# Three edits in the token-mixing part of a hybrid block: diagonal scores by a constant matrix, pooling maps inside the gate's pair, half of branch B's inputs in other tiles

## The chip, the core and the metric

The kernel runs on one core of a Trainium2 chip. The core has five engines with a queue each: TensorE (PE in the profile; its weight loads are PEld), VectorE (DVE), ScalarE (ACT), GpSimd (POOL) and SyncE (SP, which issues the transfers). Each works through its own instructions in their order and waits for the others by semaphores. The metric is device time in microseconds (us) of one execution, lower is better. Before, three timed executions took 2380.71, 2383.26 and 2383.93 us.

## The reference, cut to what matters

One layer over 1024 tokens of width 1024: a half-step FFN, a token-mixing part, a second half-step FFN and a gated embedding. The change lies in the mixing part.

```python
h = _rmsnorm(x, mix_norm[i])
proj = h @ w_in[i]
q_r, f_r, i_r, og_r, pool_r, ga_r, gb_r = jnp.split(proj, split_points, axis=-1)
f = lb + (1.0 - lb) * jax.nn.sigmoid(f_r)
k = 1.0 - f
q = jax.nn.silu(q_r)                      # 8 heads of 128
# branch A, per head:  S_t = diag(f_t) S_{t-1} + k_t outer v_t,   o_t = S_t^T q_t
o = _hgrn2_chunked(q, k, v, log_f)
o = _rmsnorm(o, hgrn_onorm[i]) * jax.nn.silu(og_r)
y_a = o @ w_branch_a[i]
# branch B: trailing means over 2/4/8/16 tokens minus the token, then a map per group of 128 channels
pooled = _causal_multiscale_pool(u)       # u: pool_r in 4 groups
mixed = jnp.einsum('bsgc,gcd->bsgd', pooled, pool_w[i]) * pool_scale[i]
y_b = mixed @ w_branch_b[i]
x = x + (jax.nn.sigmoid(ga_r) * y_a + jax.nn.sigmoid(gb_r) * y_b) @ w_out[i]
```

Within a chunk, token t's own contribution to o_t is (q_t . k_t) v_t. This number, the score of a token with itself, stands on the diagonal of the score matrix.

## The kernel before

**Arithmetic.** Every f32 operand of a large product is split into a rounded part and a remainder (`split`, line 117: a cast on ACT, line 118, and a subtraction on DVE, line 119). A product is three matmuls of 128x512 (`mm3`, lines 157 to 159: high by high, high by low, low by high). Names that end in h and l are the two parts.

**Pairs.** Two weight blocks that meet the same activations are multiplied together by a seven-product scheme (`pair`). Its weight parts are `wa` (from tile `ra`, loaded), `ws` (sums `s` made on POOL, lines 90 and 93), `wd` and `wt` (from `rb`, loaded and then overwritten by POOL). The order on PE is: products 1 and 2 (24 matmuls, into banks pA and pC, with `wa`), the two products that the pair before left over (`flushed`), then 6, 5 and 7 into pA, pB and pA. Behind product 7, ACT copies pA (line 386) and DVE adds pB (line 81). A pair takes 84 matmuls.

**Pools.** SBUF tiles come from pools: `a` (28 tiles 128x1024, activation parts), `w` (12 tiles, weights and their parts, means and pooling parts), `q`, `u` and `h` (smaller). PSUM has three banks pA, one pB, one pC and three `aux`. A tile that is asked for waits until the one whose place it takes has been read for the last time.

**Heads.** For each of 8 heads, `hgrn(h, half)` (line 916) works on two halves of 512 tokens, in 12 groups of small PE work (scores of a token with itself at line 930; scores of blocks of 1, 2, 4 ... 64 tokens at line 946, with q and k multiplied by running products of f on DVE between them; transposes of v and k at 977 and 986; the state at 994; the output at 1015 and 1017). Then the head's output is normed: squares on ACT (1020), `rstd` (a sum on DVE, a power on POOL, lines 168 and 169), a multiplication on DVE (1022). The groups of a head are interleaved with the pairs that run beside it (`among`): each head has two or three pairs beside it, and these define how many matmuls lie between two groups. `head(h)` takes the first step of `hgrn` only when head h begins.

**What is ordered by whom.** PE's order is the order of the program (`manual_schedule`). The queues of the other engines are ordered by the tile scheduler when the kernel is built.

**Pooling.** Beside heads 0 and 2, `pool_pair` makes two groups' inputs, `beside_means` makes the trailing means on DVE beside the next pair, and `pool_maps` (line 875) multiplies each of four blocks with its 128x128 map (`pb` by `pwhl`, three matmuls each, into `aux`), scales it on ACT and stores it to `m_dram`. After that comes the gate's pair `gate_pair`.

**Branch B.** `act_b` (line 1089) loads the four mixed groups back into tiles `m` and splits them into eight `a` tiles; `branch_b` multiplies them during the end of head 7 and after it; and `load_act` loads the heads' outputs and makes the activation parts (x0, x3, xT1, xT3) for branch A's pairs, also in `a` tiles.

Of the kernel before, what the change touches and what calls it, by code (L numbers as in the profile page):

```python
# [9 lines left out]
F32R = mybir.dt.float32r  # L10
# [4 lines left out]
ALU = mybir.AluOpType  # L15

P = 128
# [6 lines left out]
HEADS = 8  # L24
# [13 lines left out]
def hybrid_block(ctx: ExitStack, tc: tile.TileContext, a: dict, out: bass.AP):  # L38
# [16 lines left out]
    nc = tc.nc  # L55
# [11 lines left out]
    def t_(tag, s, dt=F32):  # L67
        n, bufs = ROOM[tag]
        return sb.tile([P, n], dt, tag=tag, name=name(s), bufs=bufs)

    def bank(tag, s=None):
        return psum.tile([P, HALF], F32, tag=tag, name=name(s or tag), bufs=BANKS[tag])
# [13 lines left out]
    def mul(o, x, y):  # L86
        nc.vector.tensor_tensor(o, x, y, ALU.mult)
# [10 lines left out]
    mhalf = small("mhalf", [P, NT])  # L98
    nc.vector.memset(mhalf, -0.5)
    masks = {}  # L100
    for h in LEVELS[:5]:

        n = 64 // h
        m = small(f"mask{h}", [P, n], BF16)
# [16 lines left out]
    def hilo(src, tag, s):  # L121

        n = src.shape[1]
        hi, lo = t_(tag, s + "h", F32R)[:, :n], t_(tag, s + "l", F32R)[:, :n]
        split(src, hi, lo)
        return hi, lo

    def hilo_half(src, tag, s):

        t = t_(tag, s, F32R)  # L130
        n = src.shape[1]
        hi, lo = t[:, :n], t[:, HALF : HALF + n]
        split(src, hi, lo)
        return hi, lo

    def halves(hl, m=HALF):

        n = hl[1].shape[1] // m
        return [(hl[0][:, c], hl[1][:, c]) for c in (slice(i * m, (i + 1) * m) for i in range(n))]
# [12 lines left out]
    def store(dst, src):  # L152
        latest[0] = nc.sync.dma_start(out=dst, in_=src).ins

    def mm3(ps, ah, al, bh, bl, first, last):
        kw = {"skip_group_check": True}
        nc.tensor.matmul(ps, ah, bh, start=first, stop=False, **kw)  # L157
        nc.tensor.matmul(ps, ah, bl, start=False, stop=False, **kw)  # L158
        nc.tensor.matmul(ps, al, bh, start=False, stop=last, **kw)  # L159

    def chunks(t, n=4):
        return [t[:, c * P : (c + 1) * P] for c in range(n)]
# [239 lines left out]
    def steps(it, n=9):  # L402
        for end in it:
            n -= end
            if not n:
                return
# [234 lines left out]
    def two_halves(s, n):  # L641
# [3 lines left out]
    ga_dram, gb_dram, yb_dram, y_dram = (  # L645
        two_halves(s, KC) for s in ("ga_dram", "gb_dram", "yb_dram", "y_dram")
    )
    m_dram = two_halves("m_dram", NG)
# [9 lines left out]
    ps = bank("pA")  # L658
# [28 lines left out]
    parts, gp = [], []  # L687
# [65 lines left out]
    pscale = load(small("pscale", [P, NG]), a["pool_scale"])  # L753
# [4 lines left out]
    Q, F, V, OG, PU, GA, GB = 0, 8, 16, 24, 32, 36, 44  # L758
    heads = {}

    def qf_pair(h):
        qk, f = [t_("q", "qk") for _ in range(2)], [t_("u", "f") for _ in range(2)]
        heads[h] = qk, f

        made = set()

        def k_(half):
            if half in made:
                nc.scalar.activation(qk[half][:, R], f[half], AF.Copy, scale=-1.0, bias=1.0)
            made.add(half)  # L770

        def q_(half):
            def go(q):
                k = qk[half][:, R]
                nc.scalar.activation(k, q, AF.Sigmoid)
                mul(q, q, k)
                k_(half)
            return go

        def f_(half):  # L780
            def go(src):
# [55 lines left out]
    def beside_means(it):  # L837

        for part in it:
            yield part  # L840
            while means and next(means[0], 0) == 0:
                means.pop(0)
        while means:
            for _ in means.pop(0):
                pass
# [29 lines left out]
    def pool_maps():  # L875

        r = t_("h", "pwr")
        load(r.rearrange("p (g d) -> p g d", g=NG), a["pool_w"].rearrange("g c d -> c g d"))
        wh, wl = hilo_half(r, "w", "pwhl")
        todo = [(g, half, u[half]) for g, u in pooled for half in range(2)]  # L880
        pooled.clear()
        parts = [hilo_half(u, "w", "pb") for _, _, u in todo[:3]]
        for _ in range(5):
            yield False
        for i, (g, half, u) in enumerate(todo):
            gc = slice(g * P, (g + 1) * P)
            if i + 3 < len(todo):
                parts.append(hilo_half(todo[i + 3][2], "w", "pb"))
            ps = bank("aux")
            mm3(ps, wh[:, gc], wl[:, gc], *parts.pop(0), True, True)  # L890
            nc.scalar.mul(u, ps, pscale[:, g : g + 1])
            store(m_dram[g][half], u)
            yield False

    def pool_pair(g):
        got = {}

        def done(i, half, t, src):
            if src is not t:
                nc.scalar.copy(t, src)  # L900
            got[i, half] = t
            for k in range(2):
                if (k, 0) in got and (k, 1) in got:
                    means.append(pool_means(g + k, [got.pop((k, 0)), got.pop((k, 1))]))

        yield from out_pair(w_in[PU + g], w_in[PU + g + 1], act, done)
# [9 lines left out]
    def hgrn(h, half):  # L916
# [5 lines left out]
        qk, f = heads[h][0][half], heads[h][1][half]  # L922
        q, k = qk[:, L], qk[:, R]
        qc, kc = chunks(q), chunks(k)
        sc = scores[half]
        yield

        ps = bank("aux")
        for p_, k_, q_ in zip(chunks(ps), kc, qc):
            nc.tensor.matmul(p_, k_, q_, start=True, stop=True)  # L930
        mul(q, q, f)
        nc.vector.copy_predicated(
            sc, ident.bitcast(U32).unsqueeze(1).to_broadcast([P, 4, P]),
            ps.rearrange("p (c t) -> p c t", c=4),
        )

        tots = {1: f}
        tot = t_("h", "tot")
        for hh in LEVELS:
            yield  # L940
            n = 64 // hh
            ps = bank("aux").rearrange("p (c x) -> p c x", c=4)
            m = 64 if hh == 64 else P
# [6 lines left out]
            by = view(tots[hh], 0, [[1, 2], [2, na], [0, hh]])  # L950
# [24 lines left out]
        ps = bank("aux")  # L975
# [8 lines left out]
        ps = bank("aux")  # L984
# [52 lines left out]
    GROUPS = 12  # L1037
    turns = []

    def head(h):  # L1040

        two = [hgrn(h, half) for half in range(2)]
        for it in two:
            next(it)
        for i in range(GROUPS):
            for it in two:
                next(it, None)
            if i in (1, 2) and turns:
                turns.pop(0)()
            yield  # L1050

    def among(its, groups, n):

        parts = (p for it in its for p in it if not p)
        done = 0
        for i, _ in enumerate(groups, 1):
            while done * GROUPS < i * n:
                next(parts, None)
                done += 1
        for k, _ in enumerate(parts):  # L1060
            if k in (1, 4) and turns:
                turns.pop(0)()
# [3 lines left out]
    def around(first, acts, *its):  # L1066
        yield first
        next(acts)
        for it in its[:-1]:
# [2 lines left out]
        yield its[-1]  # L1072

    more = {
        0: lambda: (pool_pair(0), beside_means(qf_pair(1)), pool_maps(),
                    gate_pair(GB, 0, gb_dram)),
        2: lambda: (pool_pair(2), beside_means(qf_pair(3)), pool_maps(),
                    gate_pair(GB, 2, gb_dram)),
        4: lambda: (qf_pair(5), gate_pair(GB, 4, gb_dram), gate_pair(GB, 6, gb_dram)),
        6: lambda: (qf_pair(7), gate_pair(GA, 0, ga_dram), gate_pair(GA, 2, ga_dram)),  # L1080
        7: lambda: around(gate_pair(GA, 4, ga_dram), act_b(), gate_pair(GA, 6, ga_dram), flushed(),
# [1 line left out]
    }  # L1083
    for it in (v_pair(0), qf_pair(0), og_pair(0)):
        steps(it)

    m_parts = []

    def act_b():
        behind[0] = latest[0]  # L1090
        for g in range(NG):
            m = t_("q", "m")
            for half, c in enumerate((L, R)):
                load(m[:, c], m_dram[g][half])
            m_parts.append(halves(hilo(m, "a", "m")))
        m_last, behind[0] = latest[0], None
        yield True
        behind[0] = m_last
        yield True

# [13 lines left out]
    with tc.manual_schedule(engines={nc.tensor.engine}):  # L1114
        for h in range(HEADS):
            its = more[h]() if h in more else (v_pair(h + 1), qf_pair(h + 1), og_pair(h + 1))
            among(its, head(h), (66 if h == 7 else 3 * PAIR + 9 * (h in (0, 2))))
        while turns:
            turns.pop(0)()
    behind[0] = og_last[0]  # L1120
# [275 lines left out]
```

## Time and profile before

| | |
|---|---|
| time, median of three | 2383.26 us (2380.71 to 2383.93) |
| the profiled execution's own time | 2379.58 us |
| its span | 2377.9 us |
| PE busy | 97% of the span |
| DVE, ACT, POOL busy | 61%, 41%, 19% |
| mean granted TensorE clock | 0.993 |
| diagonal scores (line 930), PE records | 128, 15.6 us busy |

A row of a timeline reads: start in us from the span's start, duration in us, engine, line, operation, out<-in, shapes, how many instructions the row holds, and in brackets how long the engine had been idle before it and what ended that. A matmul's duration is modelled and overlaps the next one's, so the pace is read from the starts. A row of a group of instructions ends with busy us and mean ns, then the idle time before them with its releasers. A row of the windows reads: from:to, length, busy us (count), granted clock, share of the DMA engines, GB/s.

### The profile page before, as it was taken

To read this page: it belongs to the slowest core of one execution; us is meant where nothing else is said; L and a number is where in the kernel's file an instruction comes from. 1 tells how busy PE (TensorE), PEld (TensorE's weight loads), DVE (VectorE), ACT (ScalarE), POOL (GpSimd) and SP (SyncE) were. 2 spreads that over 40 slices of the span, in tenths; PEclk is the share of its full clock that TensorE was granted. 3 is DMA by queue.
4 is the path that set the end of the run, shared out by engine and by line. 5 is a ranking of instruction groups with operands and counts; after the bars stand their busy time and mean duration, and the time that the engine had idled before them with its cause. 6 is when DMAs were issued, how large, how long until landed. Compare 5 with 4: busy or idle time off the path is not lost.

```text
span 2377.9 us, 29405 instructions
## 1 busy us (share of the span) xinstructions
PE 2311.8 (97%) x11058; PEld 1915.3 (81%) x11058; DVE 1457.7 (61%) x2037; ACT 980.3 (41%) x1528; POOL 442.8 (19%) x397
## 2 busy tenths in 40 slices
PE   8999999999999999999999998999999999999997
PEld 6778887888877888788888887877787888888886
DVE  6555555467656766676557567677454544568568
ACT  7344333333554333333433343346333333334656
POOL 1333222200012132122222202102223222000000
PEclk9999999999999999999999999999999999999999
DMA  4345444493431232232232366761343523754334
GB/s 183 133 139 174 152 167 140 139 347 108 138 122 58 77 106 72 80 98 84 80 99 76 98 229 230 259 229 45 109 148 124 182 93 107 263 212 131 102 97 151
DMA packets 133759, 331.75 MB, mean 140 GB/s; under 512 B 15216, under 2 KB 16240, under 8 KB 133616
## 3 DMA queue, kind: packets, MB, share of 16 engines
q1 hardware_dynamic: 133616, 329.87, 40.6%
q8 instruction: 87, 1.43, 0.3%
q14 instruction: 56, 0.46, 0.1%
HBM read 228.62 MB, written 101.19 MB: 139 GB/s over the span
## 4 chain that ended last, share of the span: by engine, by line
PE 71%; DVE 10%; DMA 7%; ACT 4%; issue 4%; POOL 4%; SPq 1%; POOLq 0%; DVEq 0%; ACTq 0%
PE pA L157 11%; PE pA L159 11%; PE pA L158 11%; PE pB L157 5%; PE pB L158 5%; PE pB L159 5%; PE aux L946 4%; PE pC L159 3%; PE pC L157 3%; PE pC L158 3%; PE aux L158 2%; PE aux L159 2%; PE aux L157 2%; DMA rb<-in_ffn_w_dram 2%; POOL s L90 1%
## 5 line engine op out<-in xcount | busy, mean ns | idle before, releaser
L90 POOL TENSOR_TENSOR s<-rb 128x512 f32<-128x512 f32 x74 | 99.5, 1344 | 836.5 <-DMA rb<-in_ffn_w_dram 352.4
L119 DVE TENSOR_TENSOR wtl<-rb,wth 128x1024 fp32r<-128x1024 f32 x74 | 90.7, 1225 | 169.3 <-ACT wth L118 169.3
L118 ACT CAST wsh<-s 128x1024 fp32r<-128x1024 f32 x74 | 77.9, 1053 | 233.9 <-POOL s L93 192.4
L119 DVE TENSOR_TENSOR wsl<-s,wsh 128x1024 fp32r<-128x1024 f32 x74 | 90.9, 1229 | 122.4 <-ACT wsh L118 122.4
L93 POOL TENSOR_TENSOR rb<-ra,s 128x512 f32<-128x512 f32 x74 | 96.4, 1303 | 341.9 <-DVE wd L119 328.6
L118 ACT CAST wth<-rb 128x1024 fp32r<-128x1024 f32 x74 | 77.7, 1050 | 194.5 <-POOL rb L93 191.1
L119 DVE TENSOR_TENSOR wal<-ra,wah 128x1024 fp32r<-128x1024 f32 x74 | 91.5, 1238 | 94.9 <-PE pC L158 50.8
L118 ACT CAST gh<-gr 128x1024 fp32r<-128x1024 f32 x84 | 81.8, 981 | 144.0 <-PE aux L158 86.3
L119 DVE TENSOR_TENSOR gl<-gr,gh 128x1024 fp32r<-128x1024 f32 x84 | 94.9, 1133 | 71.7 <-ACT gh L118 69.5
L118 ACT CAST wah<-ra 128x1024 fp32r<-128x1024 f32 x74 | 77.7, 1051 | 127.7 <-DMA ra<-in_ffn_w_dram 96.7
L157 PE MATMUL pA<-xT3h,wth 128*128 128x512 f32 x296 | 117.7, 398 | 10.6 <-ACT g L383 8.0
L157 PE MATMUL pA<-xT1h,wsh 128*128 128x512 f32 x280 | 112.0, 400 | 9.4 <-ACT xT1h L118 7.4
L157 PE MATMUL pB<-xT1h,wsh 128*128 128x512 f32 x296 | 118.2, 399 | 2.8 <-DVE o L81 1.1
L157 PE MATMUL pA<-x0h,wah 128*128 128x512 f32 x296 | 118.1, 399 | 0.8 <-ACT x0h L118 0.8
L158 PE MATMUL pA<-x0l,wah 128*128 128x512 f32 x296 | 115.7, 391 | 2.0 <-DVE x0l L119 2.0
L157 PE MATMUL pB<-x,wth 128*128 128x512 f32 x296 | 117.2, 396 | 0.0
L159 PE MATMUL pA<-xT3h,wtl 128*128 128x512 f32 x296 | 116.0, 392 | 0.5 <-DVE wtl L119 0.5
L158 PE MATMUL pB<-xT1l,wsh 128*128 128x512 f32 x296 | 116.1, 392 | 0.3 <-DVE xT1l L119 0.3
L159 PE MATMUL pB<-xT1h,wsl 128*128 128x512 f32 x296 | 116.2, 393 | 0.0
L158 PE MATMUL pA<-xT3l,wth 128*128 128x512 f32 x296 | 116.1, 392 | 0.0
L159 PE MATMUL pA<-x0h,wal 128*128 128x512 f32 x296 | 115.6, 391 | 0.0
L159 PE MATMUL pC<-x0h,wal 128*128 128x512 f32 x296 | 115.4, 390 | 0.0
(342 smaller groups left out, 6538.9 us busy)
## 6 DMA issues: line engine op xcount, KB each, us to landing
ra<-in_ffn_w_dram SPq DMA_DIRECT2D x47, 512.0 KB, 3.7
rb<-in_ffn_w_dram SPq DMA_DIRECT2D x44, 512.0 KB, 3.7
gsS<-gs SPq DMA_DIRECT2D x88, 256.0 KB, 2.2
rB<-in_ffn_w_dram SPq DMA_DIRECT2D x40, 512.0 KB, 6.8
gr<-gsS SPq DMA_DIRECT2D x40, 512.0 KB, 3.4
gsA<-g SPq DMA_DIRECT2D x66, 256.0 KB, 2.0
gr<-gsA SPq DMA_DIRECT2D x30, 512.0 KB, 5.8
ra<-in_w_in_dram SPq DMA_DIRECT2D x27, 512.0 KB, 3.7
```

What stands on the lines that cost most here:

```text
L90: nc.gpsimd.tensor_tensor(o, x, y, ALU.add)
L93: nc.gpsimd.tensor_tensor(o, x, y, ALU.subtract)
L118: nc.scalar.copy(hi, src)
L119: nc.vector.tensor_tensor(lo, src, hi.bitcast(F32), ALU.subtract)
L157: nc.tensor.matmul(ps, ah, bh, start=first, stop=False, **kw)
L158: nc.tensor.matmul(ps, ah, bl, start=False, stop=False, **kw)
L159: nc.tensor.matmul(ps, al, bh, start=False, stop=last, **kw)
L946: nc.tensor.matmul(ps[:m, c, :64], kc[c][:, :m], right, start=True, stop=True)
```

## The change

It has three parts.

1. **Diagonal scores.** Before, four 128x128 products k^T q in f32 per half gave all pairs of tokens, of which the diagonal was taken. Now DVE multiplies −2 q by k element by element (`tot`), splits that, and two 128x512 matmuls with a 128x128 matrix of −0.5 (one column of `mhalf`, broadcast) sum it over the 128 channels, so that every row holds the diagonal. This step and the first multiplication of q by f now stand in `hgrn`'s first step, and `begin_head` takes this step for head h+1 in the last group of head h (for head 0 ahead of all heads).
2. **Pooling maps.** All four blocks are split at once, and the maps are now multiplied inside the gate's pair, behind its first 24 matmuls (`maps_beside`). Scaled blocks go to tiles `mo` of the `w` pool.
3. **Branch B's inputs.** Two of the four groups are split into `w` tiles in place of `a` tiles.

```diff
@@ pool_maps
-        wh, wl = hilo_half(r, "w", "pwhl")
         todo = [(g, half, u[half]) for g, u in pooled for half in range(2)]
         pooled.clear()
-        parts = [hilo_half(u, "w", "pb") for _, _, u in todo[:3]]
-        for _ in range(5):
-            yield False
-        for i, (g, half, u) in enumerate(todo):
-            gc = slice(g * P, (g + 1) * P)
-            if i + 3 < len(todo):
-                parts.append(hilo_half(todo[i + 3][2], "w", "pb"))
-            ps = bank("aux")
-            mm3(ps, wh[:, gc], wl[:, gc], *parts.pop(0), True, True)
-            nc.scalar.mul(u, ps, pscale[:, g : g + 1])
-            store(m_dram[g][half], u)
+        parts = [hilo_half(u, "w", "pb") for _, _, u in todo]
+        wh, wl = hilo_half(r, "w", "pwhl")
+        ms = [m for _ in range(2) for m in halves((t_("w", "mo"),) * 2)]
+        yield
+        for (g, half, _), hl in zip(todo, parts):
+            gc = slice(g * P, (g + 1) * P)
+            ps = bank("aux")
+            mm3(ps, wh[:, gc], wl[:, gc], *hl, True, True)
+            m = ms.pop(0)[0]
+            nc.scalar.mul(m, ps, pscale[:, g : g + 1])
+            store(m_dram[g][half], m)
             yield False
+    def maps_beside(it):
+        maps = pool_maps()
+        next(maps)
+        done = 0
+        for part in it:
+            yield part
+            done += not part
+            if part and done == 8:
+                yield from maps
@@ hgrn
+        tot = t_("h", "tot")
+        nc.vector.scalar_tensor_tensor(tot, q, -2.0, k, ALU.mult, ALU.mult)
+        hi, lo = hilo_half(tot, "w", "qkk")
+        mul(q, q, f)
         yield
         ps = bank("aux")
-        for p_, k_, q_ in zip(chunks(ps), kc, qc):
-            nc.tensor.matmul(p_, k_, q_, start=True, stop=True)
-        mul(q, q, f)
+        by = mhalf[:, :1].bitcast(F32R).to_broadcast([P, P])
+        kw = {"skip_group_check": True}
+        nc.tensor.matmul(ps, by, hi, start=True, stop=False, **kw)
+        nc.tensor.matmul(ps, by, lo, start=False, stop=True, **kw)
@@ head
+    begun_heads = {}
+
+    def begin_head(h):
+        begun_heads[h] = [hgrn(h, half) for half in range(2)]
+        for it in begun_heads[h]:
+            next(it)
+
     def head(h):
-        two = [hgrn(h, half) for half in range(2)]
-        for it in two:
-            next(it)
+        two = begun_heads.pop(h)
         for i in range(GROUPS):
...
+            if i == GROUPS - 1 and h + 1 < HEADS:
+                begin_head(h + 1)
             yield
@@ more
-        0: lambda: (pool_pair(0), beside_means(qf_pair(1)), pool_maps(),
-                    gate_pair(GB, 0, gb_dram)),
+        0: lambda: (pool_pair(0), beside_means(qf_pair(1)),
+                    maps_beside(gate_pair(GB, 0, gb_dram))),
@@ act_b
             for half, c in enumerate((L, R)):
                 load(m[:, c], m_dram[g][half])
-            m_parts.append(halves(hilo(m, "a", "m")))
+            ms.append(m)
         m_last, behind[0] = latest[0], None
+        m_parts.extend(halves(hilo(m, "a", "m")) for m in ms[:2])
         yield True
+        m_parts.extend(halves(hilo(m, "w", "m")) for m in ms[2:])
```

Head 2's line changes as head 0's does, and the count of parts beside heads 0 and 2 goes from 3 x 28 + 9 to 3 x 28 + 4. Line numbers behind the edits move by up to 14: 946 becomes 960, 986 becomes 1000, 994 becomes 1008, 1020 becomes 1034, 1022 becomes 1036, and 932 becomes 947.

The edits change the queues of the other engines too. Three places follow; a row is line, operation, out<-in, shape.

DVE's queue at the start of head 0, before: `wal` belongs to the first pair beside head 0 (`wal_6032`), `o_5495` is the output of the pair ahead of it, `qk` and `f` are the two halves' q, k and f.

```order
L119 TENSOR_TENSOR wal_6032<-ra_6029,wah_6031 128x1024
L783 TENSOR_SCALAR f_5492<-f_5492,lb_126,lb 128x512
L87 TENSOR_TENSOR qk_5490<-qk_5490 128x512
L783 TENSOR_SCALAR f_5491<-f_5491,lb_126,lb 128x512
L119 TENSOR_TENSOR wsl_6041<-s_1189_6037,wsh_6040 128x1024
L119 TENSOR_TENSOR wd_6044<-rb_6035,wd_6044 128x512
L119 TENSOR_TENSOR wtl_6050<-rb_6035,wth_6049 128x1024
L81 TENSOR_TENSOR o_5495<-o_5495,pB_5963 128x512
L87 TENSOR_TENSOR qk_5489<-qk_5489,f_5491 128x512
L932 COPY_PREDICATED score_5481<-ident,aux_6009 128x512
```

The same place now:

```order
L81 TENSOR_TENSOR o_5495<-o_5495,pB_5963 128x512
L938 SCALAR_TENSOR_TENSOR tot_6007<-qk_5489 128x512
L938 SCALAR_TENSOR_TENSOR tot_6013<-qk_5490 128x512
L87 TENSOR_TENSOR o_5495<-o_5495,sg_6003 128x512
L119 TENSOR_TENSOR qkk_6009<-tot_6007,qkk_6009 128x512
L87 TENSOR_TENSOR qk_5489<-qk_5489,f_5491 128x512
L119 TENSOR_TENSOR qkk_6015<-tot_6013,qkk_6015 128x512
L87 TENSOR_TENSOR qk_5490<-qk_5490,f_5492 128x512
L947 COPY_PREDICATED score_5481<-ident,aux_6021 128x512
L947 COPY_PREDICATED score_5482<-ident,aux_6025 128x512
L87 TENSOR_TENSOR tot_6007<-f_5491 128x256
L119 TENSOR_TENSOR wal_6036<-ra_6033,wah_6035 128x1024
```

The products `tot` and their remainders stand behind the sum of `o`, and `wal` of the first pair has moved from ahead of all these to behind the two masked copies of the diagonal.

ACT's queue around the maps of head 2, before: `pb` and `pwhl` are the parts of the means and of the map, `wah`, `wsh` and `wd` belong to the gate's pair, L978 and L987 are the copies of v and k after their transposes, L891 scales a map.

```order
L118 CAST pb_7738<-o_7298 128x512
L118 CAST pb_7741<-o_7299 128x512
L891 ACTIVATE o_7301<-aux_7744,pscale 128x512
L118 CAST wah_7786<-ra_7784 128x1024
L978 COPY v_7466<-aux_7750 128x512
L978 COPY v_7476<-aux_7756 128x512
L891 ACTIVATE o_7300<-aux_7762,pscale 128x512
L891 ACTIVATE o_7298<-aux_7768,pscale 128x512
L891 ACTIVATE o_7299<-aux_7774,pscale 128x512
L118 CAST wsh_7795<-s_1445_7792 128x1024
L118 CAST wd_7799<-rb_7790 128x512
L987 COPY qk_6893<-aux_7828 128x512
```

The same place now (L992, L1001 and L890 are those copies and the scaling):

```order
L118 CAST pwhl_7755<-pwr_7741 128x512
L118 CAST wah_7766<-ra_7764 128x1024
L992 COPY v_7474<-aux_7802 128x512
L992 COPY v_7484<-aux_7808 128x512
L365 COPY o_7760<-pC_7789 128x512
L118 CAST wsh_7775<-s_1449_7772 128x1024
L830 ACTIVATE o_7760<-o_7760 128x512
L118 CAST wd_7779<-rb_7770 128x512
L1001 COPY qk_6903<-aux_7842 128x512
L1001 COPY qk_6904<-aux_7850 128x384
L118 CAST wth_7784<-rb_7770 128x1024
L890 ACTIVATE mo_7758<-aux_7830,pscale 128x512
```

Before, the maps were scaled ahead of `wsh`; now `wsh`, `wd`, the copies of k and `wth` stand ahead of the first scaling.

DVE's queue at the same place, before, where L868 makes the last of the means:

```order
L868 SCALAR_TENSOR_TENSOR o_7299<-pw_7711,o_7299 128x512
L119 TENSOR_TENSOR pwhl_7729<-pwr_7727,pwhl_7729 128x512
L119 TENSOR_TENSOR pb_7732<-o_7301,pb_7732 128x512
L119 TENSOR_TENSOR pb_7735<-o_7300,pb_7735 128x512
L119 TENSOR_TENSOR pb_7738<-o_7298,pb_7738 128x512
L119 TENSOR_TENSOR pb_7741<-o_7299,pb_7741 128x512
L119 TENSOR_TENSOR wal_7787<-ra_7784,wah_7786 128x1024
```

The same place now, with the remainder of the map behind those of the means:

```order
L868 SCALAR_TENSOR_TENSOR o_7313<-pw_7725,o_7313 128x512
L119 TENSOR_TENSOR pb_7743<-o_7315,pb_7743 128x512
L119 TENSOR_TENSOR pb_7746<-o_7314,pb_7746 128x512
L119 TENSOR_TENSOR pb_7749<-o_7312,pb_7749 128x512
L119 TENSOR_TENSOR pb_7752<-o_7313,pb_7752 128x512
L119 TENSOR_TENSOR pwhl_7755<-pwr_7741,pwhl_7755 128x512
L119 TENSOR_TENSOR wal_7767<-ra_7764,wah_7766 128x1024
```

`wal` of the gate's pair follows them as it did before; what moved is PE's first use of it, from behind the maps to ahead of them.

More of the change, by code (lines that the diff above doesn't have):

```diff
@@ L937, in hgrn @@
         tots = {1: f}
-        tot = t_("h", "tot")
         for hh in LEVELS:
@@ L1074, in hybrid_block @@
     more = {
-        0: lambda: (pool_pair(0), beside_means(qf_pair(1)), pool_maps(),
-                    gate_pair(GB, 0, gb_dram)),
-        2: lambda: (pool_pair(2), beside_means(qf_pair(3)), pool_maps(),
-                    gate_pair(GB, 2, gb_dram)),
+        0: lambda: (pool_pair(0), beside_means(qf_pair(1)),
+                    maps_beside(gate_pair(GB, 0, gb_dram))),
+        2: lambda: (pool_pair(2), beside_means(qf_pair(3)),
+                    maps_beside(gate_pair(GB, 2, gb_dram))),
         4: lambda: (qf_pair(5), gate_pair(GB, 4, gb_dram), gate_pair(GB, 6, gb_dram)),
@@ L1085, in hybrid_block @@
         steps(it)
+    begin_head(0)
     m_parts = []
@@ L1090, in act_b @@
         behind[0] = latest[0]
+        ms = []
         for g in range(NG):
@@ L1116, in hybrid_block @@
             its = more[h]() if h in more else (v_pair(h + 1), qf_pair(h + 1), og_pair(h + 1))
-            among(its, head(h), (66 if h == 7 else 3 * PAIR + 9 * (h in (0, 2))))
+            among(its, head(h), (66 if h == 7 else 3 * PAIR + 4 * (h in (0, 2))))
         while turns:
```

## Prediction

> **What bounds the kernel now.** I read the page's span and busy shares first.
>
> ```profile
> span 2377.9 us, 29405 instructions
> PE 2311.8 (97%) x11058; PEld 1915.3 (81%) x11058; DVE 1457.7 (61%) x2037; ACT 980.3 (41%) x1528; POOL 442.8 (19%) x397
> ```
>
> PE is busy in all but 66 us of the span. A matmul removed is therefore time won, and a wait of PE that an edit adds is time lost in full, unless it was waiting there already. So after the count of matmuls the question is which of PE's operands come late in the new order. Next I read PE's timeline at the start of head 0.
>
> ```profile
> 775.11 0.39 PE L159 MATMUL pA<-xT3h,wtl 128*128 128x512 f32 x1
> 775.34 1.95 PE L930 MATMUL aux<-qk 128*128 128x128 f32 x16
> 777.04 0.48 PE L157 MATMUL pA<-x0h,wah 128*128 128x512 f32 x1
> 777.35 0.40 PE L158 MATMUL pA<-x0l,wah 128*128 128x512 f32 x1
> 777.58 0.39 PE L159 MATMUL pA<-x0h,wal 128*128 128x512 f32 x1
> ```
>
> A 128x512 matmul follows the one before after 0.23 us. The 16 records of L930 hold PE for 1.70 us, and the matmul behind them takes 0.08 more than that pace.
>
> **Edit 1, the diagonal scores.** Out go 1.78 us in each of 8 heads; in come four matmuls of 0.227 us, so 0.91: **−7.0**. Weights that are one column read 128 times stand in no row of before. From below, they can't beat the pace, for which each product still streams 512 columns. From above, if they ran like L930 (1.70 us for 1024 columns), a head's 2048 columns would take 3.4 us, 20 us more over all heads. I take the pace, for the nearest rows in type and width have it, and keep the 20 as the far end.
>
> The price stands in the queues. The four matmuls need the new product `tot`, its cast (ACT) and its remainder (DVE), and each engine works through its queue in order. Head 0 first, with the rows of ACT and DVE there, and the group of `wal`:
>
> ```profile
> 777.59 0.58 ACT L386 COPY o<-pA 128x512 f32<-128x512 f32 x1
> ...
> 778.86 0.68 DVE L81 TENSOR_TENSOR o<-o,pB 128x512 f32<-128x512 f32 x1
> 779.46 0.69 DVE L87 TENSOR_TENSOR qk<-qk,f 128x512 f32<-128x512 f32 x1
> 780.06 0.75 DVE L932 COPY_PREDICATED score<-ident,aux 128x512 f32<-128x512 uint32 x1
> ```
>
> ```profile
> L119 DVE TENSOR_TENSOR wal<-ra,wah 128x1024 fp32r<-128x1024 f32 x74 | 91.5, 1238 | 94.9 <-PE pC L158 50.8 <-ACT wah L118 30.3 <-issue 8.4
> ```
>
> In the new order DVE's sum of `o` with pB stands ahead of both products `tot`. That sum waits for ACT's copy of pA, and the copy for PE's matmul at 775.11, the one directly ahead of the diagonal. So PE has to stop. The matmul is done at 775.5, the copy at 776.2; then the sum and seven more DVE operations of 512 at 0.60 each (the step from 778.86 to 779.46) reach 781.0, two masked copies, which now stand ahead of `wal` and wait for the diagonal itself, some 782.3, a first total 782.6, and `wal` with its 1.24 us 783.9. PE needs `wal` for the third matmul behind the diagonal, at 775.34 + 0.91 + 0.45 = 776.7. **+7.2** in head 0, in pieces of about 2.9, 2 and 2.3 us: before the diagonal, between its matmuls, and before `wal`. In before `wal` lay ahead of all this, and nothing waited.
>
> At the other seven starts `wal` of the head's first pair has moved behind both norms of the head before:
>
> ```profile
> 855.00 0.17 DVE L168 TENSOR_SCALAR rso<-rso 128x4 f32<-128x4 f32 x1
> ...
> 856.30 0.69 DVE L1022 TENSOR_TENSOR qk<-aux,rso 128x512 f32<-128x512 f32 x1 [1.02 <-POOL rso L169]
> ...
> 857.48 1.95 PE L930 MATMUL aux<-qk 128*128 128x128 f32 x16
> ...
> 931.11 0.17 DVE L168 TENSOR_SCALAR rso<-rso 128x4 f32<-128x4 f32 x1 [3.17 <-ACT qk L1020]
> ...
> 936.33 1.95 PE L930 MATMUL aux<-qk 128*128 128x128 f32 x16
> ...
> 1021.85 0.16 DVE L168 TENSOR_SCALAR rso<-rso 128x4 f32<-128x4 f32 x1
> ...
> 1024.98 1.95 PE L930 MATMUL aux<-qk 128*128 128x128 f32 x16
> ```
>
> Behind the first `rso` now stand POOL's power (1.3 us from `rso` to norm), the norm, a remainder (0.6 each), a total (0.4), the second power and norm (1.3 and 0.6), five small totals (0.6 in all) and `wal` (1.2): 6.6 us. PE wants `wal` 1.36 us after the diagonal begins. In head 2 that is 5.22 + 1.36 = 6.6 us after `rso`: 0.2 us of waiting at most, and DVE's idle 3.17 us ahead of `rso` take up the new operations that stand before it; heads 4 to 7 begin alike. In head 1 there are only 2.48 + 1.36 = 3.8 us. The queue ahead of its `rso` loses `wsl` and `wal` and gains five operations of 0.6, and I let `rso` come 0.3 earlier: +2.5. Head 3 has 3.13 + 1.36, so +1.7. With 0.2 for the other five, **+5.2** (from 0 to 12).
>
> **Edit 2, the pooling maps.**
>
> ```profile
> 992.59 0.62 ACT L118 CAST pb<-o 128x512 fp32r<-128x512 f32 x1 [0.48 <-DVE o L868]
> 993.07 2.49 DVE L119 TENSOR_TENSOR pb<-o,pb 128x512 fp32r<-128x512 f32 x4
> 993.81 0.80 PE L158 MATMUL aux<-pb,pwhl 128*128 128x512 f32 x1 [3.86 <-DVE pb L119]
> ...
> 995.71 1.03 ACT L118 CAST wah<-ra 128x1024 fp32r<-128x1024 f32 x1
> ```
>
> ```profile
> 985.00:993.00 8.00, 4.87 (x31) 1.00 0.36 116
> 993.00:1000.00 7.00, 6.19 (x19) 0.52 0.46 152
> ```
>
> ```profile
> 827.44 0.39 PE L157 MATMUL aux<-pb,pwhl 128*128 128x512 f32 x1
> ```
>
> (In the windows the second number is PE's busy time, the one behind the count its granted clock.) PE's wait of 3.86 us in head 2 goes, and the clock of 0.52 behind it, at which 6.19 us were spent on matmuls that need half: **−3.9 and −3.0**. But the gate's own matmuls now stand where the first map stood, and their `wah` and `wal` stand in ACT's and DVE's queues behind the casts and remainders of the means. In head 2 the last mean ends at 992.6. ACT then casts pb, pwhl and `wah` (to 994.7); DVE makes the five remainders at 0.60 and `wal` (to 996.7). PE's third matmul wants `wal` at 989.9: **+6.85**, first 5.3 and then 1.5. In head 0 the means are early, but `wah` waits behind the copy of `f`, whose product has just ended at 827.4: 0.6 + 1.05 + 1.24 us, less 0.45 for two matmuls that need `wah` alone: **+2.55**.
>
> Then the maps. Between them stand the transposes of k, and the copies that free their banks stand in ACT's queue behind `wsh`, a gate value and `wd` of the gate's pair:
>
> ```profile
> 999.87 1.28 POOL L90 TENSOR_TENSOR s<-rb 128x512 f32<-128x512 f32 x1 [37.91 <-DMA rb<-in_w_in_dram]
> ...
> 1002.55 1.05 ACT L118 CAST wsh<-s 128x1024 fp32r<-128x1024 f32 x1 [1.56 <-POOL s L93]
> ```
>
> Tile `s` takes the place that `wah` gives back, so POOL can begin only when the gate's first 24 matmuls end. From there `wsh` comes after 2.7 us (999.87 to 1002.55), the first copy after 2.0 more, and takes 0.5: 5.2. PE has 1.6 us of work by then (two maps, four transposes): a wait of 3.6. The second copy adds 0.6. The fourth map's bank waits for the first scaled map, which stands behind `wth` on ACT, which waits for POOL's last sum, and that for `wd`: 1.5. Together 5.7 in each of two heads: **+11.4** (from 0 to 14). The 24 matmuls ahead are no cover, since the chain begins with their end.
>
> **Edit 3, branch B's inputs.**
>
> ```profile
> 1456.53 0.50 PE L157 MATMUL pA<-x0h,wah 128*128 128x512 f32 x1 [0.81 <-ACT x0h L118]
> ...
> 1458.59 0.50 PE L158 MATMUL pA<-x0l,wah 128*128 128x512 f32 x1 [1.55 <-DVE x0l L119]
> ...
> 1463.58 0.50 PE L157 MATMUL pA<-xT3h,wsh 128*128 128x512 f32 x1 [1.71 <-DVE o L81]
> ...
> 1469.11 0.50 PE L158 MATMUL pA<-xT3l,wsh 128*128 128x512 f32 x1 [1.70 <-DVE xT3l L119]
> ```
>
> ```profile
> 1440.48 0.45 SPq L149 DMA_DIRECT2D rb<-in_w_branch_a_dram  x1
> ```
>
> These 5.8 us and 0.3 for xT1l between them end when four `a` tiles are free. In their place `rb` stands behind one more store in SP's queue, some 1.4 us later; `wsh`, `wd` and `wth` move with it, and the copy of pC stands behind `wth` on ACT, so that the sum which frees pA ends at about 1460.6, where PE is at 1458.5: +2.1. Left is **−4.0** (from −1.5 to −6).
>
> **The clock.** Before has another drop, in this place:
>
> ```profile
> 747.20 0.79 PE L157 MATMUL pA<-xT1h,wsh 128*128 128x512 f32 x1 [2.46 <-ACT xT1h L118]
> ```
>
> ```profile
> 747.00:751.00 4.00, 3.80 (x10) 0.57 0.38 100
> ```
>
> A wait of 2.46 us was enough for about 4 us at 0.57, which costs some 1.5 us. Head 0's start, head 2's gate and both rows of maps wait as long in the new order: **+6** for the four (from 0 to 12, with a second stretch behind each). The Trainium skill, "TensorE: Matmul & The Clock Gate", section "HAM oscillation", asks for "no PE-idle gaps >~3.4µs". This trace has a drop after 2.46, so here the measurement decides; by the rule the term would be about 3.
>
> **Sum**, on the profiled 2379.58: −7.0 −4.0 −3.9 −3.0 +7.2 +5.2 +6.85 +2.55 +11.4 +6.0 = +21.3, so 2400.9. That execution lies 3.7 below the median of the three timed ones; I add 1.5 for this: **2402.4**.
>
> **Rivals.** (1) The new work is ready before PE: then the savings alone are left, −17.9, about 2364. For it speaks DVE's 61% busy; against it, that in head 0 the chain hangs on PE's own last matmul. It decides if `wal` ends before 776.7 there and before 989.9 in head 2. Chance 0.14. (2) The maps find their banks: if `s` needn't wait for `wah`, 11.4 goes and half the clock's term with it: 2388. 0.11. (3) Only the longest wait drops the clock, as the 3.86 did, so head 2's gate would and the others wouldn't, save for parts of the maps: term 3, 2399. 0.09. (4) The broadcast weights run like L930: 2422. 0.04. The forecast has 0.62.
>
> **Numbers.** A measurement can tell about 0.2%, 4.8 us. Faster by more: 0.14, from (1). Within: 0.07, from (2), whose 2388 lies at the edge. Slower: 0.79. The range goes from 2378, which leaves out (1) alone, up to 2417, where clock and starts reach for their upper ends.
>
> **What would show it.** Right: PE idle for some 3 and 2 us at head 0's first L945 and L946; 5 us before the gate's first matmul in head 2, released by `wah`; waits before the transposes (L1000) and the last map; none over a microsecond for x0 and xT3 at the end of the mix. Wrong: L945 and the maps without waits, or L945 above 0.25 us apiece.

## The result, and the profile after

| | before | after |
|---|---|---|
| time, median of four | 2382.77 us (2380.71 to 2383.93) | 2441.42 us (2438.61 to 2443.18) |
| ratio | | 1.0249, 95% interval 1.0235 to 1.0262 |
| span of the profiled execution | 2377.9 us | 2441.5 us |
| mean granted TensorE clock | 0.993 | 0.981 |

The change made the kernel 58.7 us slower. The direction was forecast, the size was not: +19, and at most +34, had been expected. The page of the changed kernel begins like this (busy us, share of the span, instructions):

```profile
span 2441.5 us, 29225 instructions
PE 2331.4 (95%) x10962; PEld 1921.5 (79%) x10962; DVE 1490.5 (61%) x2069; ACT 986.3 (40%) x1544; POOL 443.0 (18%) x397
```

PE has 96 instructions fewer in the records and is busy for 20 us longer, and the span has grown by 64. So PE waits more, and it runs part of the time at a lower clock. The timeline of head 0's start, which answers to the first rows of the prediction:

```profile
776.94 0.51 PE L945 MATMUL aux<-qkk,mhalf 128*128 128x512 f32 x1 [2.65 <-ACT qkk L118]
778.09 0.49 PE L946 MATMUL aux<-qkk,mhalf 128*128 128x512 f32 x1 [0.65 <-DVE qkk L119]
...
779.29 0.79 PE L946 MATMUL aux<-qkk,mhalf 128*128 128x512 f32 x1 [0.47 <-DVE qkk L119]
...
782.58 0.80 PE L159 MATMUL pA<-x0h,wal 128*128 128x512 f32 x1 [1.64 <-DVE wal L119]
```

These are the three pieces that were foreseen: a wait before the diagonal, waits between its matmuls, one for `wal`; 5.4 us in all. The start of head 4 was to cost 0.2 us. The timeline of all engines there:

```profile
1141.93 1.29 POOL L90 TENSOR_TENSOR s<-rb 128x512 f32<-128x512 f32 x1
1141.99 0.69 DVE L1036 TENSOR_TENSOR qk<-aux,rso 128x512 f32<-128x512 f32 x1 [0.90 <-POOL rso L169]
...
1142.60 3.44 DVE L87 TENSOR_TENSOR tot<-tot 128x64 f32<-128x64 f32 x4
1142.93 0.40 PE L945 MATMUL aux<-qkk,mhalf 128*128 128x512 f32 x1
...
1143.30 1.29 POOL L93 TENSOR_TENSOR s<-s,ra 128x512 f32<-128x512 f32 x1
...
1144.55 1.26 POOL L93 TENSOR_TENSOR rb<-ra,rb 128x512 f32<-128x512 f32 x1
1146.07 0.16 DVE L87 TENSOR_TENSOR lbr<-tot 128x4 f32<-128x4 f32 x1
1146.15 1.23 DVE L119 TENSOR_TENSOR wal<-ra,wah 128x1024 fp32r<-128x1024 f32 x1
...
1147.43 0.50 PE L159 MATMUL pA<-x0h,wal 128*128 128x512 f32 x1 [2.95 <-DVE wal L119]
```

Four small totals of f, of 64, 32, 16 and 8 elements, take 3.44 us, and they take them while POOL makes its three sums. Behind them stands `wal`, and PE waits 2.95 us for it. The waits for `wal` at the starts of heads 1 to 7 are 2.51, 2.95, 3.49, 2.95, 3.45, 2.95 and 3.33 us, 21.6 together. The granted clock there, by windows of 3.4 us (from:to, length, then busy us of PE, weight loads, DVE, ACT and POOL, granted clock, DMA share, GB/s):

```profile
1141.10:1144.50 3.40, 3.39 (x15) 2.44 (x13) 2.47 (x3) 0.59 (x1) 3.32 (x3) 1.00 0.00 0
1144.50:1147.90 3.40, 0.47 (x2) 0.43 (x3) 3.30 (x6) 0.00 (x0) 1.31 (x2) 1.00 0.00 0
1147.90:1151.30 3.40, 3.40 (x10) 2.62 (x9) 3.11 (x5) 2.09 (x3) 0.00 (x0) 0.50 0.14 52
1151.30:1154.70 3.40, 3.40 (x19) 2.87 (x18) 0.75 (x2) 1.05 (x1) 1.29 (x1) 1.00 0.07 25
```

A window in which PE idles for 2.93 us is followed by one at half clock. PE's timeline there shows the pace:

```profile
1148.94 0.63 PE L157 MATMUL pA<-x0h,wah 128*128 128x512 f32 x1
1149.37 0.63 PE L158 MATMUL pA<-x0l,wah 128*128 128x512 f32 x1
```

Matmuls start 0.43 us apart in place of 0.23, so about half of such a window is lost, some 1.6 us. In the mixing part the clock is at a half for 20 such windows, against 3 before. Last, the gate of head 2, its maps, and the end of the mix, from PE's timeline:

```profile
1017.97 0.80 PE L157 MATMUL pA<-x0h,wah 128*128 128x512 f32 x1 [5.36 <-ACT wah L118]
...
1033.63 0.55 PE L1000 MATMUL aux<-ident,qk 128*128 128x128 f32 x3 [3.34 <-ACT qk L1001]
1034.74 0.50 PE L157 MATMUL aux<-pb,pwhl 128*128 128x512 f32 x1 [0.57 <-ACT qk L1001]
...
1037.05 0.80 PE L157 MATMUL aux<-pb,pwhl 128*128 128x512 f32 x1 [1.06 <-ACT mo L890]
...
1522.74 0.50 PE L157 MATMUL pA<-xT3h,wsh 128*128 128x512 f32 x1 [4.51 <-DVE o L81]
```

The gate's 5.4 us and the maps' 3.3, 0.6 and 1.1 are near what was forecast (5.3; 3.6, 0.6 and 1.5). The wait of 4.5 us for `o`, where branch A begins, was to be 2.1.

### The profile page after: what moved, and what is told of

The parts are those of the page before. It is cut to its first block, busy times and chain, and to the rows that moved or that the text cites. A ratio compares the mean times of both kernels' runs of the same rounds, so it can differ in the third digit from the quotient of the medians.

```text
span 2441.5 us, 29225 instructions
## 1 busy us (share of the span) xinstructions
PE 2331.4 (95%) x10962; PEld 1921.5 (79%) x10962; DVE 1490.5 (61%) x2069; ACT 986.3 (40%) x1544; POOL 443.0 (18%) x397
## 4 chain that ended last, share of the span: by engine, by line
PE 68%; DVE 11%; DMA 8%; ACT 4%; issue 4%; POOL 4%; SPq 1%; POOLq 0%; DVEq 0%; ACTq 0%
PE pA L157 11%; PE pA L159 11%; PE pA L158 10%; PE pB L157 5%; PE pB L158 5%; PE pB L159 5%; PE aux L960 4%; PE pC L159 3%; PE pC L157 3%; PE pC L158 3%; DMA rb<-in_ffn_w_dram 2%; PE aux L157 2%; PE aux L159 2%; PE aux L158 2%; POOL s L90 1%
## 5 line engine op out<-in xcount | busy, mean ns | idle before, releaser
L159 PE MATMUL pA<-x0h,wal 128*128 128x512 f32 x296 | 121.1, 409 | 24.6 <-DVE wal L119 24.6
L157 PE MATMUL pC<-x0h,wah 128*128 128x512 f32 x296 | 119.1, 402 | 0.0
L158 PE MATMUL pC<-x0l,wah 128*128 128x512 f32 x296 | 118.5, 400 | 0.0
L157 PE MATMUL pA<-xT3h,wd 128*128 128x512 f32 x280 | 113.1, 404 | 3.6 <-ACT c L386 2.6
```

## Experiments

Each was timed against the kernel before on the same chip, whose own median lay between 2378 and 2381 us there. Ratios are to that kernel, with their 95% intervals.

### The three edits, one at a time

`e1_diag_alone` is the kernel before with the first edit and nothing else:

```diff
+        nc.vector.scalar_tensor_tensor(tot, q, -2.0, k, ALU.mult, ALU.mult)
+        hi, lo = hilo_half(tot, "w", "qkk")
+        mul(q, q, f)
...
+            if i == GROUPS - 1 and h + 1 < HEADS:
+                begin_head(h + 1)
```

> The kernel before with the diagonal scores of the change alone (edit 1). Theory A (from the profile of the changed kernel: 5.4 us of waits at the start of head 0, 21.6 us for wal at the other seven starts, and about ten stretches of 3.4 us at half clock, less 7 us of matmuls): 2410 to 2425 us, with wal waited for 2.5 to 3.5 us in each of seven heads. Rival B (the waits at the starts of heads 1 to 7 come from the maps and branch B's tiles, which share the pool w with the parts of the product; alone, the edit costs what the forecast said, about +5): 2383 to 2393 us.

`e2_maps_alone` has the second edit only:

```diff
-        0: lambda: (pool_pair(0), beside_means(qf_pair(1)), pool_maps(),
-                    gate_pair(GB, 0, gb_dram)),
+        0: lambda: (pool_pair(0), beside_means(qf_pair(1)),
+                    maps_beside(gate_pair(GB, 0, gb_dram))),
```

> The kernel before with the maps inside the gate's pair alone (edit 2). Theory A (waits of 9.7 us at the rows of maps, 8.3 us at the gates' starts, less 3.9, and eight stretches of 3.4 us at half clock in place of two): about 2402 to 2412 us. Rival B (the gates' and maps' operands come late only because edit 1 holds DVE and ACT there): 2375 to 2388 us.

`e3_branch_b_alone` has the third:

```diff
+        m_parts.extend(halves(hilo(m, "a", "m")) for m in ms[:2])
         yield True
+        m_parts.extend(halves(hilo(m, "w", "m")) for m in ms[2:])
```

> The kernel before with half of branch B's inputs in w tiles alone (edit 3). Theory A (the splits of the heads' outputs, which now find their tiles early, stand ahead of the gb multiplications on DVE, so that yb's banks and rb come later; 4.5 us of waiting before the first pair of branch A and one stretch at half clock; the saving is eaten up): 2381 to 2388 us. The forecast's step (rb 1.4 us later): 2379 us, four less than before.

| edit | time, median | ratio | forecast for it (with its share of the clock) |
|---|---|---|---|
| 1, diagonal | 2418.12 us | 1.0160 (1.0142 to 1.0178) | +6.9 us |
| 2, maps | 2398.67 us | 1.0078 (1.0059 to 1.0097) | +18.4 us |
| 3, branch B | 2378.45 us | 0.9997 (0.9988 to 1.0006) | −4.0 us |

Before had 2378.97 us on this chip, so the edits give +39.2, +19.7 and −0.5, which add up to 58.3 of the 58.7 of the whole. The times in the expectations go by the 2383 us of before on the first chip; as differences to before, all three runs lie where Theory A had them (+27 to +42, +19 to +29, and −2 to +5). Edit 2's time came out as forecast, its terms less so (below). The loss that was not forecast is in edit 1, some 32 us, with the waits for `wal` at the seven starts also when it is alone (2.94 to 3.46 us). It needs neither the maps nor the other tiles.

### What makes `wal` late at heads 1 to 7

`e4_totals_behind` leaves the changed kernel as it is, but queues the totals behind the masked copy on DVE. This sets an order and adds no wait:

```diff
-        nc.vector.copy_predicated(
+        cp = nc.vector.copy_predicated(
...
-            mul(tots[2 * hh], pv[:, :, 0], pv[:, :, 1])
+            with tc.issue_after(cp.ins):
+                mul(tots[2 * hh], pv[:, :, 0], pv[:, :, 1])
```

> The changed kernel, with the totals of f queued on DVE behind the masked copies of the diagonal, so that they are no longer ahead of wal. Theory A (each small total on DVE waits for one of POOL's three sums, so that four totals take 3.4 us in place of 0.9, and this is nearly all of the 2.95 to 3.5 us that PE waits for wal): wal is waited for under 1.2 us at heads 1 to 7, and the time falls by 15 to 33 us, to 2408 to 2426 us. Rival B (wal is late by the two powers and norms ahead of it and by its own cast, whatever the totals do): the waits stay within 0.8 us of 3, and the time within 8 us of 2441.

Measured: 2406.93 us, ratio 1.0112 (1.0097 to 1.0128), against the changed kernel's 1.0249, a difference of 33 us and the far end of what Theory A expected (15 to 33). The start of head 4 in this run:

```profile
1127.98 1.70 DVE L119 TENSOR_TENSOR wal<-ra,wah 128x1024 fp32r<-128x1024 f32 x1
...
1128.67 2.16 POOL L93 TENSOR_TENSOR s<-s,ra 128x512 f32<-128x512 f32 x1
...
1130.18 0.39 PE L159 MATMUL pA<-x0h,wal 128*128 128x512 f32 x1
```

PE no longer waits for `wal` at the start of any of heads 1 to 7, and no window at half clock is left there. `wal` (1.70 us against 1.23) and POOL's second sum (2.16 against 1.29) still lengthen each other, but there is time for it.

This run takes the totals away from `wal` as well as from POOL's sums. `e5_sums_behind_wal` holds the other side fixed: DVE's queue is that of the changed kernel, instruction by instruction, and POOL's sums come later.

```diff
+            if fresh:
+                fresh.clear()
+                lo = w["A11"][1].bitcast(F32)
+                held = nc.gpsimd.tensor_tensor(dummy, lo[:, :1], lo[:, :1], ALU.add).ins
+                with tc.issue_after(held):
+                    pool_add(s[:, L], rb[:, L], rb[:, R])
...
                 begin_head(h + 1)
+                fresh.append(True)
```

> The changed kernel with DVE's queue left as it is, totals ahead of wal, but POOL's sums of the first pair of heads 1 to 7 made to wait for wal (a one-column sum on POOL that reads wal stands ahead of them). Theory A (DVE's totals and POOL's sums hold each other up): with nothing on POOL beside them the four totals take about 0.9 us again, wal is waited for under 1 us, some waiting moves to wsh (0 to 2 us a head, since POOL now starts later), and the time is 2405 to 2430 us. Rival B (the queue ahead of wal is simply long): the waits for wal stay at 2.5 to 3.5 us and the time at 2436 us or more.

Measured: 2410.03 us, ratio 1.0120 (1.0106 to 1.0134). Head 4's start in its timeline (L120 and L160 are the lines 119 and 159 of the changed kernel):

```profile
1128.23 1.23 DVE L120 TENSOR_TENSOR wal<-ra,wah 128x1024 fp32r<-128x1024 f32 x1
...
1129.52 0.50 PE L160 MATMUL pA<-x0h,wal 128*128 128x512 f32 x1 [0.37 <-DVE wal L120]
1129.54 0.19 POOL L349 TENSOR_TENSOR dummy<-wal 128x1 f32<-128x1 f32 x1 [2.92 <-DVE wal L120]
```

The waits for `wal` are 0.35 to 0.48 us, with all totals ahead of it as they were. Waits for `wsh`, which might have come up in their place, did not. So the queue's length accounts for 0.4 us of some 3; the rest is DVE and POOL holding each other up. Here too the half clock at these starts is gone: 18.9 us of waits and 12.5 of clock (worked out below) make 31.4, and the run is some 31 below the changed kernel by the ratios. The groups of two of the totals show how DVE and POOL hold each other up, over all 16 halves, first before, then the changed kernel, then this run (busy us and mean ns behind the bar):

```profile
L87 DVE TENSOR_TENSOR tot<-tot 128x32 f32<-128x32 f32 x16 | 3.4, 227 | 0.2
L87 DVE TENSOR_TENSOR tot<-tot 128x64 f32<-128x64 f32 x16 | 3.2, 219 | 0.2
```

```profile
L87 DVE TENSOR_TENSOR tot<-tot 128x32 f32<-128x32 f32 x16 | 10.7, 673 | 0.5
L87 DVE TENSOR_TENSOR tot<-tot 128x64 f32<-128x64 f32 x16 | 8.8, 553 | 0.1
```

```profile
L87 DVE TENSOR_TENSOR tot<-tot 128x64 f32<-128x64 f32 x16 | 4.5, 288 | 0.1
L87 DVE TENSOR_TENSOR tot<-tot 128x32 f32<-128x32 f32 x16 | 4.1, 259 | 0.5
```

### Edit 1 alone, mended

`e6_diag_totals_behind` is e1 with the two lines of e4.

> The kernel before with edit 1 alone and the totals behind the masked copies. Theory A (all of edit 1's loss at heads 1 to 7 is the totals; head 0 keeps 5.4 us of waits and about 3.4 us of clock against 1.5 before; the matmuls save 7): within 4 us of before, on either side. Rival B (the clock's drops and later queues cost more than the waits themselves): 10 us or more above before.

Measured: 2384.73 us against 2381.09, ratio 1.0012 (1.0001 to 1.0023). The waits at heads 1 to 7 are gone, as in e4. Head 0 keeps its waits of 2.65, 0.66, 0.25 and 1.64 us, and they and the half clock behind them (three windows, some 4 us) eat up the 7 us of matmuls. `e7_diag_head0_early` takes head 0's first step inside the output gate's pair (`og_pair`), which runs ahead of head 0:

```diff
         while leads:
-            steps(leads.pop(0))
+            for i, _ in enumerate(leads.pop(0)):
+                if not leads and hook and i == 9:
+                    hook.pop()()
...
+    hook.append(lambda: begin_head(0))
     for it in (v_pair(0), qf_pair(0), og_pair(0)):
         steps(it)
-    begin_head(0)
```

> As the run before, and head 0's first step taken inside the output gate's pair, once q, k and f of head 0 are there, so that its product, cast and remainder stand ahead of the sum of o on DVE. Theory A (head 0's wait is only the order of DVE's queue): no wait over 0.6 us at head 0's diagonal or for wal behind it, no half clock there, and 5 to 9 us less than before (the 7 us of matmuls are won). Rival B (the tot operations delay that pair's own sums or wal): waits of 1 us or more come up there, and the time is within 3 us of the run before.

Measured: 2376.47 us, ratio 0.9984 (0.9972 to 0.9995), 8.3 us below e6 on the same chip. Head 0 in its timeline:

```profile
770.93 0.40 PE L939 MATMUL aux<-qkk,mhalf 128*128 128x512 f32 x1
...
772.85 0.50 PE L159 MATMUL pA<-x0h,wal 128*128 128x512 f32 x1 [0.36 <-DVE wal L119]
```

Of the four waits 0.36 us is left. The gain on before is 4.6 us, a little under the 5 to 9 expected.

`e8_maps_after_weights` puts the maps into that kernel's gate pair, but splits the means only after the gate's weights, and multiplies the maps after both rows of k's transposes:

```diff
+            trues += part
+            if part and trues == 2:
+                next(maps)
+            if not part and done == 20:
+                yield from maps
```

> As the run before, with the maps inside the gate's pair, but the means split only after the gate's weights, and the maps multiplied behind product 6, after both rows of k's transposes. Theory A (the maps cost what they did because the gate's weights stood behind the means' parts and the copies of k behind wsh): no wait of over 1 us at the transposes or maps; head 2's gate still waits 3 to 4 us for wal, which stands behind the last mean; the time is within 4 us of the run before. Rival B (the maps cost by their place in the pools whatever the order): 8 us or more above the run before.

Measured: 2379.71 us, ratio 0.9994 (0.9983 to 1.0004), 3.2 us above e7. From PE's timeline:

```profile
842.02 0.50 PE L157 MATMUL pA<-xT1h,wsh 128*128 128x512 f32 x1 [1.54 <-DVE o L81]
...
993.77 0.79 PE L157 MATMUL pA<-x0h,wah 128*128 128x512 f32 x1 [4.82 <-ACT wah L118]
```

The waits at the transposes and maps are down to 0.25 us, as Theory A had it, so they came from the order and not from the pools. The run moves the splits on ACT and DVE and the maps on PE together; which of these did it is not shown. Head 2's gate still waits, by 4.8 us and for `wah` where a wait of 3 to 4 for `wal` was expected, and 1.5 us came up in head 0. The maps' old stall of 3.86 us is thus only moved. The intervals of e7 and e8 overlap, so the 3.2 us between them are not clear of noise.

### Why edit 3 gained nothing

In e3 PE waits 4.30 us for `o` at the start of branch A, in place of the 6.1 us for x0, xT1, xT3 and `o` before. SP's queue and DVE's there:

```profile
1440.35 0.43 SPq L149 DMA_DIRECT2D ra<-in_w_branch_a_dram  x1
...
1445.15 0.32 SPq L153 DMA_DIRECT2D yb_dram<-gb  x1
...
1447.70 0.32 SPq L153 DMA_DIRECT2D yb_dram<-gb  x1
1448.11 0.39 SPq L149 DMA_DIRECT2D rb<-in_w_branch_a_dram  x1
```

```profile
1443.83 0.69 DVE L84 TENSOR_TENSOR b<-b,b 128x512 f32<-128x512 f32 x1 [1.89 <-DMA b<-o_dram]
1444.44 0.69 DVE L87 TENSOR_TENSOR gb<-yb,gb 128x512 f32<-128x512 f32 x1
```

The splits of the heads' outputs now find their tiles early, so their subtractions (L84) stand early in DVE's queue and wait there for loads. The product `gb` behind them comes late, SP stands in the store of that product, and `rb` is issued 40.2 us behind branch B's first matmul; before it was 33.5. The next run issues these stores from POOL's queue:

```diff
-            store(yb_dram[j][half], gb)
+            nc.gpsimd.dma_start(out=yb_dram[j][half], in_=gb)
```

> The kernel before with edit 3 alone, and the stores of yb issued from POOL's queue in place of SP's. Theory A (edit 3 gains nothing because SP stands in two yb stores that wait for gb products queued on DVE behind the new early splits, so that rb is issued 7.6 us later than before): rb is issued within 2 us of where it was before (33.5 us behind the first yb matmul), the wait of 4.3 us for o ahead of branch A's pair falls under 2 us, and the time is 3 to 7 us below before. Rival B (the pair waits for places of w tiles or for DVE's splits, whichever queue stores): the wait stays at 3.5 us or more and the time within 2 us of before.

Measured: 2376.78 us against 2377.88, ratio 0.9999 (0.9990 to 1.0008). `rb` comes 30.7 us behind the first matmul, even 2.8 earlier than before, and the wait for `o` is gone. But there is a new one:

```profile
1437.12 0.50 PE L157 MATMUL yb<-mh,wb 128*128 128x512 f32 x1 [2.08 <-DVE gb L87]
```

PE waits 2.08, 0.44 and 0.22 us for `gb` within branch B itself, and 1.35 us for one of ACT's copies at 1483.81, where it did not wait before. So each theory is half right: the store held up `rb`, and lifting that alone does not bring the 3 to 7 us. That the rest is lost to the same order on DVE is argued from this row; it was not tried.

`e10_diag_and_b` is e7 with edit 3 and these stores.

> Edit 1 with the totals behind the masked copies and head 0's first step early (as in e7), and edit 3 with the stores of yb on POOL's queue. Theory A (both savings add up): 3 to 7 us below e7, 8 to 13 us below before. Rival B (the wait for o stays, or POOL's stores delay its sums): within 2 us of e7.

Measured: 2372.52 us against 2377.88, ratio 0.9974 (0.9965 to 0.9982). That is 5.4 us below before, under the 8 to 13 expected. PE waits for `gb` again (1.08, 0.27 and 2.52 us) and not for `o`. Its ratio is the lowest of these kernels, a quarter of a per cent below before; whether edit 3 adds to e7 stays open, since the two intervals overlap.

## Why the prediction was wrong

| term | forecast, us | in the two traces, us |
|---|---|---|
| diagonal's matmuls | −7.0 | −7.0 (four matmuls 0.23 apart) |
| head 0's start | +7.2 | +5.4, and a wait of 1.48 just ahead of it is gone |
| starts of heads 1 to 7 | +5.2 | **+21.6** |
| gates' starts, both | +9.4 | +8.3 |
| rows of maps, both | +11.4 | +9.7 |
| the maps' old stall | −3.9 | −3.9 |
| edit 3 | −4.0 | **+1.1** (−6.1; +4.5 for `o` and +2.7 for `gb`) |
| clock (half of PE's busy time at half clock) | +3.0 | **+24.3** |

With the wait of 1.48 that is gone, the right column adds up to +58.0 of the span's +63.6. Of the other 5.6 us, 4 are waits of PE after the mix, 15.6 us against 11.7, in code that the change doesn't touch; the rest is not assigned.

**The starts of heads 1 to 7: the step that failed.** It added up what stands between the first `rso` and `wal` to 6.6 us, with "five small totals (0.6 in all)". The rest of that sum was nearly right: `rso` comes 5.20 to 5.22 us before the diagonal at all seven starts, as supposed for head 2, and with 6.6 us `wal` would have been in time. In e5, where POOL is idle beside the totals, that stretch takes 7.06 us at head 4 and PE waits 0.37; in the changed kernel it takes 9.65. What failed is that the totals were taken at their cost with POOL idle, so the time in which DVE and POOL hold each other up stood at nothing. In the new order POOL's three sums of the same pair stand right behind the second power, so they run exactly while DVE makes the totals. Of the four totals behind the norm, the first three each last until the end of a sum; the four together take 3.4 to 4.0 us in heads 2 to 7. Both e4 and e5 show it, each moving one of the two sides. Head 1's forecast of 2.5 met the 2.51 by luck: there `rso` came as early as elsewhere, and the totals took 1.92 us and `wal` 2.20, both beside sums.

The trace of before carried the warning. The instructions on `tot` there, over all forms (shortest, median and longest ns):

```profile
L87 DVE TENSOR_TENSOR tot<-tot x80: 159/192/982, 783.2 to 1335.9; 128x128 f32<-128x128 f32 x16, 128x64 f32<-128x64 f32 x16, 128x32 f32<-128x32 f32 x16, 128x16 f32<-128x16 f32 x16
```

The one that takes 982 ns, where the median is 192, runs beside a POOL sum (the first of the two totals of this DVE row):

```profile
1017.34 1.72 POOL L93 TENSOR_TENSOR rb<-ra,rb 128x512 f32<-128x512 f32 x1
...
1018.11 1.19 DVE L87 TENSOR_TENSOR tot<-tot 128x16 f32<-128x16 f32 x2
```

A mean of a group hides this; the spread shows it. The Trainium skill, "SBUF — State Buffer", section "SBUF: two separate sides", has the mechanism: DVE and GpSimd share a pair of ports as an exclusive lock, which a DVE operation with two SBUF inputs and a GpSimd operation that reads SBUF take for the whole instruction. These traces agree: totals wait for whole sums of 1.29 us, while the norm `qk<-aux,rso`, whose one input is in PSUM, keeps its 0.69 beside POOL.

**The clock** was the larger sum of the miss, +24 for +3. Of the cost, 12.5 us belong to the seven starts whose waits were not foreseen. At the four places that were foreseen (head 0's start, head 2's gate and both rows of maps) half clock cost 11.4 us against the 6 given: the forecast counted one stretch at each, and there were two or three. Head 0's gate and the start of branch A, which it left out, cost 1.7 each; 3.0 of before are gone.

**Edit 3** was mis-sized in the step on `rb`. "Some 1.4 us later" for one more store became 6.7 us in e3 and 9.3 in the changed kernel, since the stores themselves waited for DVE. The savings on x0 and xT3 came as forecast, and the 2.7 us for `gb` were not foreseen.

**What held:** the matmuls' price with broadcast weights, the row of pieces at head 0 and its cause (e7), the gates' starts and the waits at the maps. The sum for edit 2 held by luck: in e2 the waits, less the maps' old stall, come to 13.8 us where 16.9 were forecast, and the clock to 5.0 where it was 1.5. Rivals 1 to 4 did not occur (the savings alone would give 2363 and not 2364, which changes nothing). The range ended at 2417 because it bounded the starts of heads 1 to 7 by 12 us and the clock by 12; the trace has 21.6 and 27 there.

## What to carry to other kernels

When an edit puts DVE work ahead of something urgent, read what POOL does at that time: in these traces DVE's operations with two inputs in SBUF and POOL's sums took turns, so the price of a short one was up to the length of a sum, 1.3 us. Look at the longest of a group, not at its mean. A wait of PE of some 2 us or more inside a dense run of matmuls can cost half as much again, since the clock behind it is part of the price (12.5 us behind the 21.6 at the seven starts); and a saving of a few matmuls pays only if the operands of the very next pair aren't queued behind its preparation.

## What the runs showed of the hardware

- The half clock follows PE's idle time in fixed stretches of 3.41 us. Worked out from PE's waits and the granted clock in the twelve traces of this case (before, after, e1 to e10), without the first six stretches and the last few of each: of the full-speed stretches with 1.9 us or more of idle time, 79 of 79 were followed by half clock; of 49 with 1.5 to 1.9 us, 15; of some 8000 with less, one. A stretch at half clock was followed by another if PE idled 0.7 us or more in it (37 of 37), and almost never below 0.5 (1 of 92). The rule weighed in the prediction (the Trainium skill, "TensorE: Matmul & The Clock Gate", section "HAM oscillation") sets in at gaps of about 3.4 us; in these traces 1.9 us within a stretch was enough every time. And the same wait may cost nothing where a stretch's edge divides it. Head 1's 2.51 us did so, as the windows there show: 1.65 and 0.85 us idle in two stretches, and full clock in the third.

```profile
874.80:878.20 3.40, 1.75 (x8) 1.10 (x6) 3.25 (x6) 0.59 (x1) 2.85 (x3) 1.00 0.00 0
878.20:881.60 3.40, 2.55 (x11) 2.13 (x12) 2.69 (x4) 1.34 (x2) 1.95 (x1) 1.00 0.00 0
881.60:885.00 3.40, 3.40 (x21) 2.93 (x20) 1.82 (x2) 1.33 (x3) 1.17 (x1) 1.00 0.21 77
```

- Weights that are one column read 128 times cost no more than others: 0.23 us from one L945 or L946 to the next in each head but head 0, which has waits between them.
